# Odd mixer of a hybrid encoder: the forget gate moved into the score matmul, softmax read from PSUM, PSUM banks divided anew

## The chip, the cores and the metric

One core of a Trainium2 chip runs the whole inference step as one program. The metric is the device time of the program in microseconds; a smaller number is better. All times below are for one core, and there is no traffic with other cores.

## The reference, cut to what matters

The model is a two-layer encoder step for a prompt of 512 tokens and a sample of 32 tokens (544 columns side by side), width 1024, everything in float32. Layer 0 has a convolution and state-space mixer, layer 1 (the odd layer) has forgetting attention and a chunk gating unit, and both layers end in a convolutional FFN. The change is in the attention of layer 1: 8 heads of 64 features, in which a cumulated log forget value F is added to the scores.

```python
def fox_block(q, k, v, fq, fk, qpos, kpos):
    s = jnp.einsum('bqhd,bkhd->bhqk', q, k).astype(jnp.float32) * (C_HEAD_DIM ** -0.5)
    s = s + (jnp.transpose(fq, (0, 2, 1))[:, :, :, None] - jnp.transpose(fk, (0, 2, 1))[:, :, None, :])
    s = jnp.where((kpos[None, :] <= qpos[:, None])[None, None], s, MASK_VALUE)
    p = jax.nn.softmax(s, axis=-1)
    return jnp.einsum('bhqk,bkhd->bqhd', p.astype(v.dtype), v)

F = jnp.cumsum(logf.astype(jnp.float32), axis=1)      # logf = log_sigmoid(fl + b_forget)
```

So a score is q.k/8 + F[query] - F[key], masked to keys no later than the query. The prompt is done in blocks of 128 queries, the 32 sample queries see 256 cached keys and their own 32.

## The kernel before, in words

**Products.** Activations lie as (features on partitions, tokens on columns). Every projection goes through `phase` (L163) in jobs: one job is one block of 128 output features on one half of the tokens (256 or 288 columns), 24 matmuls at L128 to L130, because weights and activations are split into a high and a low part (float32r) and three of the four products are formed. A job writes one PSUM bank. Its result is taken out ("drained") by the phase's `consume` function, here `c_in` (L1026), one job later (lag 1). Weights come in blocks of 512 KB: `prefetch` (L91) issues the load on SP's queue (L101, `raw`, two buffers), ScalarE makes the high part `wh` (L104) and VectorE the low part `wl` (L105), four buffers each.

**PSUM.** There are eight banks. The pool `mm` holds four for jobs throughout. In the odd mixer the other four are `sc` with two (scores and other small products), `pp` with one (transposed weights) and `av` with one (weighted values). In the tail (FFN and embedding) `ps_tile` (L110) takes turns between `mm` and three more banks, and one bank serves the norms. In the even mixer the other four go to the state-space scan.

**The odd mixer** (`mixer_odd`, L992) runs 21 weight blocks: the forget logits first, then k, q, v for each of four pairs of heads, then the gating unit's inputs. Beside the jobs run the steps of the attention: `each` (L1332) advances the generator `pipe` (L1182) at a fixed rate per job. There are 16 blocks of the prompt (four pairs, each with four blocks of 128 queries, both heads together) and one block for the sample. At one turn of `pipe` PE gets the weighted values of block t-2, the scores of block t (both heads) and the transposes of the softmax of block t-1.

- `forget` (L1109) makes the log forget values of all heads on 8 partitions and scans them (L1121, L1123) to `F` and `Fs`, the negated sums of prompt and sample. `forget_cols` (L1126) turns them into columns `fq` with small matmuls (L1130, L1134).
- `row` (L1169) copies one head's row of `F` to all 128 partitions, as a DMA on SP's queue from one partition (L1173, tile `Gb`, four buffers, 256 KB each, eight in all); the sample's two `Gb` come by eight smaller ones (L1177). `pipe` issues a row one block before its first use.
- `split_heads` (L1151) splits q or k of a pair into high and low parts (L1159 on ScalarE, L1160 on VectorE) and copies one part to the other 64 partitions with two DMAs issued on POOL (L1163).
- `Head.products` (L1213) forms a head's scores in two passes: 128 rows (q high, q low on k high, k high; L1216), then 64 rows (q high on k low; L1217).
- `Head.softmax` (L1220): VectorE adds `Gb` and the column of `fq` on the way out of PSUM (L1223), adds the mask (L1225), takes the maximum (L1142) and negates it (L1143); ScalarE does the exponential (L1144) and the scaling (L1146), VectorE the reciprocal (L1145).
- `turn` (L1228) transposes the weights (L1231) and ScalarE copies them out (L1233, `pT`, three buffers); `values` (L1235) forms the weighted sum (L1242).
- Around these: `kT` and `vT` go out as results (`out_o_k` at L1047, `out_o_v` at L1052). The gating input `VD` takes the place of `kT` (one buffer), so its first drain (L1043) waits until `out_o_k` has read `kT`. `values_t` (L1069) transposes v through `sc`; ScalarE copies it (L1075).

**Order.** Each engine and each queue works through its instructions in one fixed order. That order is written when the kernel is built, by a scheduler that follows the order of the program and its own estimate of durations, so neighbours on an engine can come from different functions. A wait at the head of an engine or queue holds all that stands behind it.

Of the kernel before, what the change touches and what calls it, by code (L numbers as in the profile page):

```python
# [31 lines left out]
# columns of the packed per-feature parameters  # L32
# [15 lines left out]
# columns of the shape-only constants  # L48
# [3 lines left out]
def units():  # L52
    """Weight blocks in the order of their use: (array, index, K tiles)."""
# [17 lines left out]
def trunk_kernel(ctx: ExitStack, tc: tile.TileContext, A: dict):  # L71
# [36 lines left out]
    psc = {"extra": None, "st": None, "n": 0}  # L108
# [13 lines left out]
    def mm_job(ps, u, ks, xh, xl, c0, n, k0=0):  # L122
        """ps[:, :n] = W.T @ x for one block: W = hi + lo, x = hi + lo."""
# [8 lines left out]
    # ------------------------------------------- work beside the products, in steps  # L132
# [30 lines left out]
    def phase(n, K, src, consume, delta=4, after=(None, None), each=None, rate=2, lag=1):  # L163
        """n weight blocks on both halves of the tokens, the first half ahead by delta."""
# [36 lines left out]
    # -------------------------------------------------------------- constants  # L201
# [15 lines left out]
    act.activation(mhalf, zero[:, 0:4], AF.Gelu_apprx_tanh)      # its table also holds the other functions  # L217
# [6 lines left out]
    # history of the FFN's convolution: [prompt's last two of the first half, cache]  # L224
# [28 lines left out]
    def history(U, half, prev, cache):  # L253
        """The columns before the first token of each block."""
# [56 lines left out]
    def split_x(k, c0, n, src, g=None):  # L311
        """X[k] = src * g in two parts."""
# [7 lines left out]
    def residual(half, h, y, st, gpost, gnext, rB=None):  # L320
        """h += y * g * r; then X of the next projection and, for rB, the norm of h."""
# [37 lines left out]
    def tail(layer, h, next_g):  # L359
        """Output projection of the mixer, FFN and per-layer embedding.  # L360

        X holds the mixer's output. Returns h and rB of the next layer's norm."""
# [3 lines left out]
        psc["extra"] = fs.enter_context(tc.tile_pool(name="fp%d" % layer, bufs=3, space=PSUM))  # L366
# [15 lines left out]
        # the sample's part of the per-layer input  # L382
# [3 lines left out]
        # FFN  # L386
# [57 lines left out]
        # per-layer embedding: half of p @ w_ple  # L444
# [62 lines left out]
    # ------------------------------------------------------- layer 0: the mixer  # L507
    def mixer_even(h):
        ms = ExitStack()
        s5 = ms.enter_context(tc.tile_pool(name="s5", bufs=1))  # L510
        aux = ms.enter_context(tc.tile_pool(name="s5p", bufs=1, space=PSUM))

# [5 lines left out]
        # until their places are filled: bb in the last quarter of Bm, raw in the one before, ct in Tm  # L518
# [11 lines left out]
        # X = h * g, the statistics of h  # L530
# [52 lines left out]
        # ---- discretization, on (2 groups x 64 states, 16 pairs of groups)  # L583
# [29 lines left out]
        def horner(r, cs):  # L613
            """r * (cs[0] + r * (cs[1] + ...))"""
# [16 lines left out]
        pw = s5.tile([128, 5, 2, 16], F32, tag="pw", name="pw")   # powers 1..4 of A  # L631
        pg = s5.tile([128, 2, 16, 3], F32, tag="pg", name="pg")   # powers 3..1, by pair of groups
# [8 lines left out]
        def cmul(o, a, b):  # L641
            """o = a * b, complex"""
# [10 lines left out]
        def discretize():  # L653
# [40 lines left out]
            # f = (A - 1) / a  # L694
# [23 lines left out]
        def rotations():  # L718
            """Powers of the unit rotation per chunk: of column m to m - 63, of the start column and the
            sample's chunks after it to 0, 1, ..."""  # L720
            et = ya.rearrange("p f t -> p (f t)")[:, 0:1024].rearrange("p (a q m) -> p a q m", a=2, q=16)
            for b in range(6):
# [3 lines left out]
                if b in (2, 4, 5):  # L726
                    # back to the unit circle: E *= (3 - |E|^2) / 2
# [22 lines left out]
        # ---- stationary matrices  # L750
# [3 lines left out]
        def prep_b(fr, fi):  # L754
            # bb = ((re, im), (-im, re)) of f * b
# [12 lines left out]
            # raw = ((c_re, -c_im), (-c_im, -c_re))  # L768
# [73 lines left out]
        # ---- chunk scan of two pairs of groups  # L842
# [68 lines left out]
        def shuffle(back_, fs):  # L911
            """Between (channels, time in chunk) and (time in chunk, 2 groups x 16 channels)."""
# [13 lines left out]
        # ---- gated convolution  # L926
# [40 lines left out]
        # ---- gate of the S5 output  # L967
# [7 lines left out]
        for jh in range(2):  # L975
            for o in range(4):
# [7 lines left out]
                for a, b, m0, m1 in ((0, SEQ, 0, 128), (S0, T, SS0, M)):  # L984
# [3 lines left out]
                    vec.scalar_tensor_tensor(xl_, tv[:, :, m0:m1], 0.5, xh_, op0=OP.mult, op1=OP.subtract)  # L988
        ms.close()

    # ------------------------------------------------------- layer 1: the mixer
    def mixer_odd(rB):  # L992
        """Attention and spatial gating."""
# [5 lines left out]
        def sc():  # L999
            return aux.tile([128, 512], F32, tag="sc", name="sc", bufs=2)  # L1000
# [11 lines left out]
        F = at.tile([8, SEQ], F32, tag="F", name="F")               # cumulated log forget, negated  # L1012
        Fs = at.tile([8, 288], F32, tag="Fs", name="Fs")
        fq = at.tile([128, 5, 8], F32, tag="fq", name="fq")
        nid = at.tile([8, 8], F32, tag="nid", name="nid")
        lfs, lf, fa, fb = [uT[0:8, j] for j in range(4)]             # until u is there
# [44 lines left out]
        def spatial():  # L1061
            """The spatial weights (rows s, columns t), of them only s <= t."""
# [6 lines left out]
        def values_t(i):  # L1069
            """v of a pair of heads: (features, tokens) -> (tokens, features)"""  # L1070
# [27 lines left out]
        def to_tokens(src, dst, dst_s, blocks):  # L1098
            """(features, tokens) -> (tokens, features), by blocks of tokens"""
# [405 lines left out]
```

## Time and profile before

| what | value |
|---|---|
| three timed runs | 1452.87, 1453.6, 1455.97 us, median 1453.6 |
| profiled execution, span from first to last instruction | 1451.2 us |
| its own time beside the span | not listed apart; the median of the runs is 2.4 us above the span |
| PE (TensorE matmul) busy | 1384.4 us, 95% |
| VectorE, ScalarE, POOL busy | 960.2, 641.3, 228.8 us |
| odd mixer, first to last job | about 697 to 940 us |

The profile is of one execution. "PE busy" counts matmuls whose ends are modelled; "granted clock" is TensorE's clock as a share of 2.4 GHz, so 0.50 is 1.2 GHz. A wait "A <- B" says that engine A stood idle until B had ended. The chain of waits is the chain of work that ended last, followed back from the end.

### The profile page before, as it was taken

What the parts mean: (1) busy time and instruction counts of PE and PEld (TensorE: products, weight loads), DVE (VectorE), ACT (ScalarE), POOL (GpSimd) and SP (SyncE); (2) the same over time, 40 slices, a digit from 0 to 9 for tenths busy, and PEclk for the clock granted to TensorE, in tenths of its full rate; (3) what the DMA queues carried; (4) which work ended last, traced back from release to release, by engine and by line L of the source; (5) the groups of instructions that cost most, each with busy time, mean ns of one, the idle gap of its engine ahead of it and who ended that gap; (6) DMA issues with size and microseconds to landing.
All of it is one profiled execution on the core that took longest, in us unless ns stands there. A gap on an engine that the chain in (4) does not pass through costs nothing.

```text
span 1451.2 us, 27530 instructions
## 1 busy us (share of the span) xinstructions
PE 1384.4 (95%) x10863; PEld 1352.1 (93%) x10863; DVE 960.2 (66%) x2051; ACT 641.3 (44%) x1268; POOL 228.8 (16%) x658
## 2 busy tenths in 40 slices
PE   8699999999999999999939979999999999999998
PEld 7698999999999999999937868999999999999998
DVE  8998748982578357678506546649881578368683
ACT  6344546552344134465405545556542344134451
POOL 2622000430023002100000000001340024003000
PEclk9899999999999999999968989999999999999999
DMA  5222352231223122241385751231231223122221
GB/s 191 76 65 69 110 184 74 81 110 64 97 83 111 64 94 70 86 139 59 79 60 57 92 146 53 91 118 58 88 131 60 73 88 131 60 73 85 95 83 52
DMA packets 50081, 130.60 MB, mean 90 GB/s; under 512 B 8080, under 2 KB 19736, under 8 KB 49696
## 3 DMA queue, kind: packets, MB, share of 16 engines
q1 hardware_dynamic: 48672, 126.74, 31.0%
q0 software_dynamic: 1280, 2.10, 0.7%
q8 instruction: 85, 1.39, 0.4%
q14 instruction: 44, 0.36, 0.1%
HBM read 116.93 MB, written 4.76 MB: 84 GB/s over the span
## 4 chain that ended last, share of the span: by engine, by line
PE 84%; DVE 8%; DMA 4%; ACT 2%; SPq 2%; issue 1%; POOL 0%; ACTq 0%; DVEq 0%; POOLq 0%
PE ps L128 26%; PE ps L130 26%; PE ps L129 26%; DMA raw<-in_w_odd_in 2%; DMA out_o_k<-kT 1%; DVE wl L105 1%; SPq L1173 1%; PE av L1242 1%; PE sc L1217 1%; PE pp L1231 1%; PE sc L1216 1%; PE rp L298 1%; DVE rg L870 1%; ACT wh L104 0%; DVE y L329 0%
## 5 line engine op out<-in xcount | busy, mean ns | idle before, releaser
L128 PE MATMUL ps<-Xh,wh 128*128 128x256 f32 (+1 forms) x2512 | 730.0, 291 | 6.2 <-DVE UUh L579 5.4
L129 PE MATMUL ps<-Xl,wh 128*128 128x256 f32 (+1 forms) x2512 | 727.6, 290 | 2.6 <-DVE Xl L318 2.4
L130 PE MATMUL ps<-Xh,wl 128*128 128x256 f32 (+1 forms) x2512 | 727.9, 290 | 2.2 <-DVE wl L105 2.2
L128 PEld LDWEIGHTS ps<-Xh,wh 128*128 128x128 f32 x2512 | 476.0, 190 | 9.5 <-issue 3.6
L129 PEld LDWEIGHTS ps<-Xl,wh 128*128 128x128 f32 x2512 | 476.4, 190 | 4.0 <-DVE Xl L318 3.0
L130 PEld LDWEIGHTS ps<-Xh,wl 128*128 128x128 f32 x2512 | 474.9, 189 | 3.3 <-DVE wl L105 2.6
L105 DVE TENSOR_TENSOR wl<-raw,wh 128x1024 fp32r<-128x1024 f32 (+1 forms) x213 | 257.3, 1209 | 183.4 <-ACT wh L104 181.7
L104 ACT ACTIVATE wh<-raw 128x1024 fp32r<-128x1024 f32 (+1 forms) x213 | 221.8, 1042 | 279.8 <-PE ps L129 227.5
L128 PE MATMUL ps<-gh,wh 128*128 128x288 f32 (+1 forms) x704 | 203.5, 289 | 0.0
L130 PE MATMUL ps<-gh,wl 128*128 128x288 f32 (+1 forms) x704 | 203.4, 289 | 0.0
L129 PE MATMUL ps<-gl,wh 128*128 128x288 f32 (+1 forms) x704 | 202.5, 288 | 0.0
L129 PEld LDWEIGHTS ps<-gl,wh 128*128 128x128 f32 x704 | 133.5, 190 | 0.0
L128 PEld LDWEIGHTS ps<-gh,wh 128*128 128x128 f32 x704 | 133.0, 189 | 0.0
L130 PEld LDWEIGHTS ps<-gh,wl 128*128 128x128 f32 x704 | 132.9, 189 | 0.0
L269 ACT ACTIVATE t<-U,prm 128x256 f32<-128x256 f32 (+1 forms) x176 | 90.1, 516 | 71.0 <-DVE U L403 67.5
L270 DVE SCALAR_TENSOR_TENSOR t<-U,prm,t 128x256 f32<-128x256 f32 (+1 forms) x176 | 87.0, 498 | 34.8 <-ACT t L269 34.5
L403 DVE TENSOR_TENSOR U<-ps,rB 128x256 f32<-128x256 f32 (+1 forms) x176 | 76.5, 436 | 24.1 <-PE ps L130 20.3
L271 DVE SCALAR_TENSOR_TENSOR t<-U,prm,t 128x256 f32<-128x256 f32 (+1 forms) x176 | 87.5, 500 | 4.6
L406 POOL COPY hca<-U 128x2 f32<-128x2 f32 x88 | 24.2, 277 | 365.3 <-DVE U L403 365.1
L413 ACT ACTIVATE t<-t 128x288 f32<-128x288 f32 (+1 forms) x88 | 37.6, 428 | 81.6 <-DVE t L271 81.5
L429 DVE TENSOR_TENSOR y<-y,ps 128x256 f32<-128x256 f32 (+1 forms) x64 | 27.9, 437 | 62.1 <-PE ps L130 62.1
L419 ACT ACTIVATE gh<-t 128x288 fp32r<-128x288 f32 (+1 forms) x88 | 37.3, 424 | 67.5 <-DVE t L417 67.5
(276 smaller groups left out, 1427.3 us busy)
## 6 DMA issues: line engine op xcount, KB each, us to landing
raw<-in_w_up SPq DMA_DIRECT2D x88, 512.0 KB, 3.5
raw<-in_w_down SPq DMA_DIRECT2D x32, 512.0 KB, 3.5
raw<-in_w_odd_in SPq DMA_DIRECT2D x21, 512.0 KB, 4.0
raw<-in_w_even_in SPq DMA_DIRECT2D x16, 512.0 KB, 3.6
raw<-in_w_gate SPq DMA_DIRECT2D x16, 512.0 KB, 4.3
raw<-in_w_down SPq DMA_DIRECT2D x16, 384.0 KB, 2.9
raw<-in_w_even_out SPq DMA_DIRECT2D x8, 512.0 KB, 3.9
raw<-in_w_odd_out SPq DMA_DIRECT2D x8, 512.0 KB, 3.5
```

The source lines that it names most:

```text
L104: act.activation(wh[:, :K], raw[:, :K], AF.Copy)
L105: vec.tensor_tensor(wl[:, :K], raw[:, :K], wh[:, :K], op=OP.subtract)
L128: pe.matmul(ps[:, :n], wh[:, k0 + k, :], h_, start=(i == 0), stop=False)
L129: pe.matmul(ps[:, :n], wh[:, k0 + k, :], l_, start=False, stop=False)
L130: pe.matmul(ps[:, :n], wl[:, k0 + k, :], h_, start=False, stop=(i == last))
L269: act.activation(t, v[2], AF.Copy, scale=w(2))
L270: vec.scalar_tensor_tensor(t, v[1], w(1), t, op0=OP.mult, op1=OP.add)
L271: vec.scalar_tensor_tensor(t, v[0], w(0), t, op0=OP.mult, op1=OP.add)
L403: vec.tensor_tensor(block_view(U, half)[2], like(ps, half), like(rB[half], half), op=OP.mult)
L413: act.activation(t, t, AF.Gelu_apprx_tanh)
L419: act.activation(gh[:, f - f0], g, AF.Copy)
L429: vec.tensor_tensor(yk, yk, ps, op=OP.add)
```

## The change

The forget values are no longer copied to all partitions. Per head, 64 partitions of a q tile and of a k tile are free in the first pass; the change puts four useful rows there: q has (F high, F low) against ones in k, and ones against (F high, F low) in k, the rest is zero. So the first pass (q high on k high, plus the gate rows) already holds F[query] - F[key], and the second pass takes both cross terms (q high on k low, q low on k high). The scores are complete in PSUM; mask, maximum and exponential read them there.

- Gone: all 16 row DMAs on SP (L1173, L1177), the addition L1223, the negation L1143 (now in the maximum), the `fq` columns of the prompt, tiles `Gb`, `kl`.
- New: four fixed tiles `QA`, `KA` (two pairs in turn) with 16 memsets on POOL at the mixer's start; `forget` also splits F in two parts twice (`FK`, `FQ`: two ScalarE and two VectorE operations on 8 partitions, written where `lf` lay, which `out_o_logf` reads); per `split_heads` two more small DMAs on POOL (one partition to two, 4 KB; 16 in all); for q two more ScalarE copies of 64x512; `forget_cols` copies the sample's rows by matmul (`Gs`).
- PSUM: `mm` three banks instead of four everywhere; `sc` three instead of two; the tail's second pool four instead of three, with the turns of `ps_tile` turned round so that seven banks still rotate; the even mixer gets one extra bank that takes each fourth job.
- `pT` two buffers instead of three; `F`, `Fs` and a selection matrix use buffers of the pool `S`.

```diff
-    mm = ctx.enter_context(tc.tile_pool(name="mm", bufs=4, space=PSUM))
+    mm = ctx.enter_context(tc.tile_pool(name="mm", bufs=3, space=PSUM))
-        p_ = psc["extra"] if psc["extra"] is not None and psc["n"] % 7 % 2 else mm
+        p_ = psc["extra"] if psc["extra"] is not None and psc["n"] % psc["of"][0] % psc["of"][1] == 0 else mm
-        psc["extra"] = fs.enter_context(tc.tile_pool(name="fp%d" % layer, bufs=3, space=PSUM))
+        psc["extra"] = fs.enter_context(tc.tile_pool(name="fp%d" % layer, bufs=4, space=PSUM))
+        psc["of"] = (7, 2)
...
+        psc["extra"] = ms.enter_context(tc.tile_pool(name="s5m", bufs=1, space=PSUM))
+        psc["of"] = (4, 4)
...
-            return aux.tile([128, 512], F32, tag="sc", name="sc", bufs=2)
+            return aux.tile([128, 512], F32, tag="sc", name="sc", bufs=3)
...
+        FQ, FK = [uT[0:8, j:j + 2, 0:SEQ].bitcast(F32R) for j in (0, 2)]
+        QA, KA = [[at.tile([128, 2, SEQ], F32R, tag="%s%d" % (n, p), name=n) for p in range(2)] for n in ("QA", "KA")]
+        for p in range(2):
+            for hh in range(2):
+                o = gate_rows(hh)
+                pool_e.memset(QA[p][o:o + 32, hh].bitcast(F32), 0.0)
+                pool_e.memset(KA[p][o:o + 32, hh].bitcast(F32), 1.0)
+                pool_e.memset(QA[p][o + 32:o + 64, hh].bitcast(F32), 1.0)
+                pool_e.memset(KA[p][o + 32:o + 64, hh].bitcast(F32), 0.0)
...
-            vec.tensor_tensor_scan(F, one.to_broadcast([8, SEQ]), x[:, 0:SEQ], 0.0, op0=OP.mult, op1=OP.subtract)
+            vec.tensor_tensor_scan(F[0:8], one.to_broadcast([8, SEQ]), x[:, 0:SEQ], 0.0, op0=OP.mult, op1=OP.subtract)
+            act.activation(FK[:, 0], F[0:8], AF.Copy)
+            vec.tensor_tensor(FK[:, 1], F[0:8], FK[:, 0], op=OP.subtract)
...
+            act.activation(FQ[:, 0], F[0:8], AF.Copy, scale=-1.0)
+            vec.tensor_tensor(FQ[:, 1], FK[:, 0], F[0:8], op=OP.subtract)
...
+            for g in range(2):
+                ps = sc()
+                pe.matmul(ps[:, 0:288], pick[:, 128 * g:128 * g + 128], Fs, start=True, stop=True)
...
+            vec.tensor_reduce(mx[:, 1:2], src[:, :n], axis=mybir.AxisListType.X, op=OP.max, negate=True)
+            act.activation(S[:, :n], src[:, :n], AF.Exp, bias=mx[:, 1:2], accum_out=mx[:, 2:3])
...
             for hh in range(2):
-                s, o = slice(hh * 64, hh * 64 + 64), slice(64 - hh * 64, 128 - hh * 64)
-                nc.gpsimd.dma_start(hi[o, hh], lo[s] if isq else hi[s, hh])
...
+                nc.gpsimd.dma_start(B[o:o + 64, hh], lo[s] if isq else A[s, hh])
+                h_ = 2 * i + hh
+                o2 = o if isq else o + 32
+                nc.gpsimd.dma_start(A[o2:o2 + 2, hh], (FQ if isq else FK)[h_:h_ + 1])
...
-        def row(key):
...
-                pe.matmul(ps[:, :n], Q2[i][:, self.hh, b * 128:n], K2[i][:, self.hh, 0:n], start=True, stop=False)
-                pe.matmul(ps[:, :n], Q2[i][s, self.hh, b * 128:n], KL[i][s, 0:n], start=False, stop=True)
+                pe.matmul(ps[:, :n], QA[i % 2][:, hh, b * 128:n], KA[i % 2][:, hh, 0:n], start=True, stop=False)
+                pe.matmul(ps[:, :n], QB[i][:, hh, b * 128:n], KB[i][:, hh, 0:n], start=False, stop=True)
...
-                vec.scalar_tensor_tensor(S[:, :n], Gb[h_][:, :n], fq[:, b, h_:h_ + 1], ps[:, :n],
-                                         op0=OP.add, op1=OP.add)
-                vec.tensor_tensor(S[:, b * 128:n], S[:, b * 128:n], mask_p, op=OP.add)
-                normalize(S, n)
+                vec.tensor_tensor(ps[:, b * 128:n], ps[:, b * 128:n], mask_p, op=OP.add)
+                normalize(S, n, ps)
```

## Rows read from the trace of the kernel before

**Rows 1.** The page's first lines: span, busy time of each engine

```profile
span 1451.2 us, 27530 instructions
...
PE 1384.4 (95%) x10863; PEld 1352.1 (93%) x10863; DVE 960.2 (66%) x2051; ACT 641.3 (44%) x1268; POOL 228.8 (16%) x658
```

**Rows 2.** Waits by engine and line, 700 to 900 us: total, times, longest

```profile
ACT wh L104 <- DMA raw<-in_w_odd_in: 32.6, 2, 32.4
...
PE sc L1216 <- ACT VT L1075: 26.2, 1, 26.2
...
DVE VD L1043 <- DMA out_o_k<-kT: 12.7, 1, 12.7
...
PE pp L1231 <- ACT pT L1233: 11.5, 1, 11.5
```

**Rows 3.** Chain that ended last, 690 to 930 us: start, length, what

```profile
726.37 9.96 SPq L1173
736.44 24.27 DMA raw<-in_w_odd_in
...
763.70 0.48 PE sc L1216
...
821.47 20.92 DMA out_o_k<-kT
...
845.01 0.47 PE pp L1231
```

**Rows 4.** What the DMA engines moved, 715 to 765 us in 40 slices

```profile
GB/s 29 341 170 134 29 26 28 26 26 26 26 33 26 26 26 28 28 26 62 129 61 41 30 29 31 29 28 43 26 28 26 28 26 26 280 243 252 82 2 267
```

**Rows 5.** Stretches: length, busy by engine (PE first), granted clock, DMA share, GB/s

```profile
770.00:771.00 1.00, 1.00 (x8) 1.00 (x8) 0.00 (x0) 0.00 (x0) 0.00 (x0) 0.73 0.00 0
...
849.00:850.00 1.00, 1.00 (x10) 0.87 (x11) 0.18 (x1) 0.00 (x0) 1.00 (x2) 0.97 0.85 283
...
864.00:866.00 2.00, 2.00 (x18) 2.00 (x18) 0.62 (x2) 1.77 (x4) 0.67 (x1) 1.00 0.78 31
```

**Rows 6.** In order of time: VectorE's first drain of VD; SP's issue of out_o_v

```profile
842.49 0.42 DVE L1043 SCALAR_TENSOR_TENSOR VD<-ps,rB 128x256 f32<-128x256 f32 x1 [12.66 <-DMA out_o_k<-kT]
...
856.28 0.34 SPq L1052 DMA_DIRECT2D out_o_v<-vT  x1
```

**Rows 7.** Groups of instructions by shape, 690 to 900 us: busy, mean ns

```profile
L1223 DVE SCALAR_TENSOR_TENSOR S<-Gb,fq,sc 128x512 f32<-128x512 f32 x8 | 5.9, 746 | 2.5 <-PE sc L1217 1.4 <-PE pp L1231 1.1
...
L1159 ACT ACTIVATE hi<-qT 64x512 fp32r<-64x512 f32 x8 | 5.0, 623 | 0.1
...
L1216 PE MATMUL sc<-hi 128*128 128x512 f32 x8 | 4.0, 498 | 0.0
L1217 PE MATMUL sc<-lo,hi 64*128 64x512 f32 x8 | 4.0, 498 | 0.0
```

**Rows 8.** PE in order of time: forget columns; scores at a pair's start

```profile
718.39 1.05 PE L1130 MATMUL sc<-nid,F 8*128 8x8 f32 x8 [0.76 <-DVE F L1121]
720.51 0.30 PE L1134 MATMUL sc<-nid,Fs 8*32 8x1 f32 x16
...
825.09 0.33 PE L1216 MATMUL sc<-hi 128*128 128x128 f32 x1
...
827.44 0.38 PE L1217 MATMUL sc<-lo,hi 64*128 64x256 f32 x1
```

**Rows 9.** POOL: the longest memset's group, then two rows in order of time

```profile
L525 POOL MEMSET Cm<- 128x5120 f32 x1 | 4.4, 4365 | 0.0
...
703.60 0.85 POOL L302 TENSOR_TENSOR rc<-mc,mhalf 128x3 f32<-128x3 f32 x1 [18.20 <-DVE mc L300]
...
725.23 0.51 POOL L1163 DMA_DIRECT2D hi<-lo  x1 [0.21 <-issue]
```

**Rows 10.** Issue to landing: the copies of L1163, then the rows of L1173

```profile
DMA to landing us min/median/max: 2.2/3.3/23.7
...
DMA to landing us min/median/max: 11.8/15.8/34.1
```

More of the change, by code (lines that the diff above doesn't have):

```diff
@@ L988, in mixer_even @@
                     vec.scalar_tensor_tensor(xl_, tv[:, :, m0:m1], 0.5, xh_, op0=OP.mult, op1=OP.subtract)
+        psc["extra"] = None
         ms.close()
@@ L1011, in mixer_odd, with gate_rows @@
         bs = at.tile([128, 4, 128], F32, tag="bs", name="bs")
-        F = at.tile([8, SEQ], F32, tag="F", name="F")
-        Fs = at.tile([8, 288], F32, tag="Fs", name="Fs")
-        fq = at.tile([128, 5, 8], F32, tag="fq", name="fq")
+        F, Fs = buf("F"), buf("Fs")[0:8, 0:288]
+        Gs = []
         nid = at.tile([8, 8], F32, tag="nid", name="nid")
+        FQ, FK = [uT[0:8, j:j + 2, 0:SEQ].bitcast(F32R) for j in (0, 2)]
+        QA, KA = [[at.tile([128, 2, SEQ], F32R, tag="%s%d" % (n, p), name=n) for p in range(2)] for n in ("QA", "KA")]
+        def gate_rows(hh):
+            return 64 - hh * 64
+        for p in range(2):
[5 more added lines that the diff above has]
+                pool_e.memset(KA[p][o + 32:o + 64, hh].bitcast(F32), 0.0)
         lfs, lf, fa, fb = [uT[0:8, j] for j in range(4)]
@@ L1124, in forget @@
                                    op0=OP.mult, op1=OP.subtract)
+            act.activation(FQ[:, 0], F[0:8], AF.Copy, scale=-1.0)
+            vec.tensor_tensor(FQ[:, 1], FK[:, 0], F[0:8], op=OP.subtract)
         def forget_cols():
             yield True
-            ps = sc()
-            for b in range(4):
-                pe.matmul(ps[:, b * 8:b * 8 + 8], F[:, b * 128:b * 128 + 128], nid,
-                          start=True, stop=True)
-            for h_ in range(8):
-                g, r = divmod(h_, 4)
-                pe.matmul(ps[32 * r:32 * r + 32, 32 + g:33 + g], Fs[:, 256:288], nid[:, h_:h_ + 1],
-                          start=True, stop=True, tile_position=(0, 32 * r))
@@ L1136, in forget_cols @@
-            act.activation(fq[:, 0:4].rearrange("p b h -> p (b h)"), ps[:, 0:32], AF.Copy)
-            act.activation(fq[:, 4, 0:2], ps[:, 32:34], AF.Copy)
+            pick = buf("pick")[0:8, 0:256]
+            act.activation(pick.rearrange("p (h q) -> p h q", q=32),
+                           ident[0:8, 0:8][:, :, None].to_broadcast([8, 8, 32]), AF.Copy)
+            for g in range(2):
+                ps = sc()
+                pe.matmul(ps[:, 0:288], pick[:, 128 * g:128 * g + 128], Fs, start=True, stop=True)
+                for r in range(4):
+                    h_ = 4 * g + r
+                    pe.matmul(ps[32 * r:32 * r + 32, 288:289], Fs[:, 256:288], nid[:, h_:h_ + 1],
+                              start=True, stop=True, tile_position=(0, 32 * r))
+                Gs.append(at.tile([128, 289], F32, tag="Gs%d" % g, name="Gs"))
+                act.activation(Gs[g], ps[:, 0:289], AF.Copy)
@@ L1145, in normalize @@
             vec.reciprocal(mx[:, 3:4], mx[:, 2:3])
             act.activation(S[:, :n], S[:, :n], AF.Copy, scale=mx[:, 3:4])
-        Gb, av = {}, {}
-        Q2, K2, KL = {}, {}, {}
+        av = {}
+        QB, KB = {}, {}
         def split_heads(i, isq):
-            hi = at.tile([128, 2, SEQ], F32R, tag="q2" if isq else "k2", name="hi", bufs=2)
-            lo = at.tile([128, SEQ], F32R, tag="S" if isq else "kl", name="lo", bufs=4 if isq else 2)
+            A, B = (QA if isq else KA)[i % 2], at.tile([128, 2, SEQ], F32R, tag="q2" if isq else "k2", name="B", bufs=2)
@@ L1156, in split_heads @@
             src = (qT if isq else kT)[:, i, 0:SEQ]
+            lo = at.tile([128, SEQ], F32R, tag="S", name="lo", bufs=4) if isq else None
             for hh in range(2):
                 s = slice(hh * 64, hh * 64 + 64)
-                act.activation(hi[s, hh], src[s], AF.Copy)
-                vec.tensor_tensor(lo[s], src[s], hi[s, hh], op=OP.subtract)
+                act.activation(A[s, hh], src[s], AF.Copy)
+                vec.tensor_tensor(lo[s] if isq else B[s, hh], src[s], A[s, hh], op=OP.subtract)
+                if isq:
+                    act.activation(B[s, hh], src[s], AF.Copy)
@@ L1161, in split_heads @@
             for hh in range(2):
-                s, o = slice(hh * 64, hh * 64 + 64), slice(64 - hh * 64, 128 - hh * 64)
-                nc.gpsimd.dma_start(hi[o, hh], lo[s] if isq else hi[s, hh])
-            if isq:
-                Q2[i] = hi
-            else:
-                K2[i], KL[i] = hi, lo
-        def row(key):
-            g = Gb[key] = at.tile([128, SEQ], F32, tag="Gb", name="Gb", bufs=4)
-            if key < 8:
-                nc.sync.dma_start(g, F[key:key + 1][:, None].to_broadcast([1, 128, SEQ]))
-            else:
-                for r in range(4):
-                    h_ = 4 * (key - 8) + r
-                    nc.sync.dma_start(g[32 * r:32 * r + 32, 0:288], Fs[h_:h_ + 1][:, None].to_broadcast([1, 32, 288]))
+                s, o = slice(hh * 64, hh * 64 + 64), gate_rows(hh)
@@ L1187, in pipe @@
                 if t < NB:
-                    for x in blocks[t]:
-                        if x.h not in Gb:
-                            row(x.h)
                     ps = [x.products() for x in blocks[t]]
@@ L1193, in pipe @@
                         x.softmax(p_)
-                    if t + 1 < len(blocks):
-                        for x in blocks[t + 1]:
-                            if x.h not in Gb:
-                                row(x.h)
                 if 1 <= t < NB + 1:
@@ L1231, in turn @@
                     pe.transpose(pp[:, k * 128:k * 128 + 128], self.S[:, k * 128:k * 128 + 128], ident)
-                self.pT = at.tile([128, SEQ], F32, tag="pT", name="pT", bufs=3)
+                self.pT = at.tile([128, SEQ], F32, tag="pT", name="pT", bufs=2)
                 act.activation(self.pT[:, :self.n], pp[:, :self.n], AF.Copy)
@@ L1266, in softmax @@
                 S = self.S = buf("S")
[L1267 removed]
+                vec.scalar_tensor_tensor(S[:, 0:288], Gs[g][:, 0:288], Gs[g][:, 288:289], ps[:, 0:288],
                                          op0=OP.add, op1=OP.add)
@@ L1275, in turn @@
                     pe.transpose(pp[:n, k * 128:k * 128 + 128], self.S[:, k * 128:k * 128 + n], ident)
-                self.pT = at.tile([128, SEQ], F32, tag="pT", name="pT", bufs=3)
+                self.pT = at.tile([128, SEQ], F32, tag="pT", name="pT", bufs=2)
                 act.activation(self.pT[:, 0:256], pp[:, 0:256], AF.Copy)
```

14 lines of the change are left out of this document (6 added, 8 removed).

## The prediction

> **What bounds the kernel now.** I read the page first. PE is busy 1384.4 of 1451.2 us [rows 1], so TensorE sets the pace, and a change to the attention's other engines can only pay where PE stands still. The next view is therefore the waits of the odd mixer. Two waits of PE stand out there [rows 2]: 26.2 us in front of the first scores (L1216) and 11.5 us in front of transposes (L1231). The line named as releaser, a ScalarE copy, is only the last link. The same view shows what held ScalarE and VectorE: ScalarE's weight split L104 waited 32.4 us for a weight load, and VectorE's first drain of `VD` waited 12.7 us for the output copy `out_o_k`.
>
> The chain of waits says why these two transfers were late [rows 3]. Before the weight load stands SP itself, held by the issue of the broadcast rows L1173 (the last of the first four took 9.96 us to issue), so the load went out only at 736.44, and then it took 24.27 us to land. What filled the DMA engines is seen in the rates [rows 4]: for most of 40 us they moved 26 to 29 GB/s, though the weight loads before and after show 243 to 341. A row copy reads one partition and lands after 11.8 to 34.1 us [rows 10]. The second case has the same pattern: two rows were issued just before `out_o_k`, which needed 20.92 us [rows 3]. So both stalls come from the broadcasts of F, through SP's queue and through the DMA engines.
>
> **The change, part by part.**
>
> *Broadcasts gone.* The four first rows no longer stand between two weight loads on SP, and nothing slow lies in front of the load. The first idle ends at 763.70 [rows 3]; it began 26.2 us earlier, at 737.5, and I take all of it as gained. The second, 11.5 us, likewise. What is late next? For the weights: PE's next job with that block cannot start before the scores that PE waited for, and an unhindered load lands in a few us, so nothing. For `out_o_k`: VectorE came to the drain at 842.49 - 12.66 = 829.83 [rows 6], that is 8.4 us after the issue at 821.47. `out_o_v`, the same size, was issued at 856.28 [rows 6] with two 512 KB loads beside it, and by 864 the rate had fallen to 31 GB/s [rows 5]; that is under 8 us. So the wait is 0 to 2 us on VectorE, and PE had other work until 833.5: nothing.
>
> *Clock.* After each idle stretch PE worked at 1.2 GHz for a while. In the slice from 770 to 771 the mean granted clock was 0.73, so full speed came at about 770.54; in that from 849 to 850 it was 0.97, so at 849.06 [rows 5]. PE ran at half clock from 763.70 to 770.54 (6.84 us) and from 845.01 [rows 3] to 849.06 (4.05 us). At full clock that work takes half: 3.4 and 2.0 us gained.
>
> *PE's own work.* The second pass contracts 128 rows instead of 64; both passes took 498 ns for 512 columns [rows 7], so nothing. `forget_cols` now needs the second scan for all its matmuls. Before, PE waited 0.76 us for the first scan, at 718.39, and came to the group that needs the second at 720.51 [rows 8]. The added wait is at most 2.1 us and at least nothing; I take 1.5, near the top, because two operations for the split of F now lie between the scans.
>
> *Softmax from PSUM.* VectorE loses L1223 (746 ns at 512 columns [rows 7]) and a one-column operation; the maximum and the mask read PSUM now, and even if each cost as much as L1223 did, no more would come back than left. ScalarE gets eight more copies at 623 ns for q [rows 7], 5.0 us in all. Over the span VectorE is busy 66% and ScalarE 44% [rows 1], so this lies beside PE's work: nothing. A bank with scores is now held until the exponential has read it, not until the first VectorE operation. The place to look is a pair's start, where four score tiles follow each other from 825.09 to 827.8 [rows 8]. The third bank takes one; the fourth tile needs the bank of the first, about 2 us after that was filled, and mask, maximum and exponential take about that. Between 0 and 1 us for each of four pairs: I take 0.5, so 2 us.
>
> For this the Trainium skill (PSUM — Partial Sum Buffer, Summary: rules for kernel authors) says to empty PSUM promptly because it is small, which speaks against reading a softmax from it. By that rule every block would wait, as in the second rival below; by the rows only pair starts do.
>
> *Banks of the jobs.* Three instead of four in the odd mixer. With lag 1 a job needs the bank of the job three before; nearly all drains start as their job ends, apart from the two stalls, and a late one has two whole jobs as cover. In tail and even mixer seven and four banks rotate as before. Nothing.
>
> *POOL.* 16 memsets of 512 columns at 4365/5120 ns per column [rows 9] are 0.44 us each, 7.0 in all. Behind them stands the norm's power at 703.60, before which POOL idled for 18.2 us [rows 9]; with the mixer's memory free at its first job, near 697, they end near 704, and that power, 0.85 us long, is wanted one job later. Nothing; were the memory free only at 703.6, up to 7.0 us. Two more DMA issues of 0.51 us [rows 9] per split put the last one for pair 0 at 725.74 + 1.0 = 726.8, still 10.7 us ahead of the scores at 737.5. VectorE's `FQ` overwrites what `out_o_logf` reads and waits for it; behind it stand drains of two jobs, covered by the third bank. Nothing.
>
> *Sum.* -26.2 - 11.5 - 3.4 - 2.0 + 1.5 + 2 = -39.6 us. The profiled span of 1451.2 becomes 1411.6; the median of the runs is 2.4 us above the span, so I forecast 1414.0 us.
>
> **Rivals.**
>
> 1. *The second stall stays*: `out_o_k` still lands late, because loads go out beside it. For: a 1 MB output and loads share the engines. Against: `out_o_v` under the same load. It keeps 11.5 + 2.0 us: 1427.5.
> 2. *Scores wait for banks at every block*: the exponential stands behind other ScalarE work, and PE waits 1 us for each of 17 blocks instead of 2 us in all. For: the longer hold. Against: after a pair's start at least a job's products lie between two blocks. It costs 15 us: 1429.
> 3. *Slower: the gate rows arrive late.* They too are read from one partition, and go through POOL's queue. If such a row landed like a broadcast, after 34.1 us [rows 10], each pair's first scores would wait, taken at pair 0's margin, 34.1 - 10.7 = 23.4 us, four times: 1414.0 + 94 = 1508. It decides from a landing of about 20.6 us on (39.6/4 = 9.9 beyond the margin). For: even a copy of L1163 once took 23.7 us. Against: that was under the broadcasts; the least is 2.2 us for 128 KB [rows 10], and a gate row has 4 KB.
> 4. *The broadcasts are not what held the transfers*, so both stalls stay: 1453.6 + 3.5 = 1457 at most, or the same as now. Against: the rates [rows 4].
>
> **How the numbers follow.** The forecast has 0.75, rival 1 0.10, rival 2 0.09, rival 3 0.03, rival 4 0.03. Low end: no added waits (-3.5), and PE's small wait of 0.76 us [rows 8] and the bubbles between a 128-row and a 64-row pass go too (some 4 us by an estimate of 0.1 us for each of 32 tiles): 1406. High end: rivals 1 and 2, 1430. About 0.1 is left out above and below. A measurement of this kernel tells 0.2%, 2.9 us, from no change. Faster by more than that: forecast, rivals 1 and 2, 0.94. Within it: 0.02. Slower: 0.04.
>
> **What would show it.** Right: no stretch of half clock between 700 and 930 us, the weight load landing in under 6 us, no wait of VectorE for `out_o_k` over 2 us, odd mixer some 40 us shorter, tails unchanged. PE's waits before the scores would be under 1 us each, and at pair starts only. Wrong: a new wait of PE for score banks or for gate rows at each pair, a wait of the job's matmuls for a bank, or tails that take longer under the new turns of the banks.

## The result, and the profile after

The changed kernel takes **1403.99 us**, median of four runs (1403.22 to 1404.62), against 1453.23 us before (four runs, 1452.81 to 1455.97): a ratio of 0.9657, with a 95% interval of 0.9643 to 0.967. Its profiled execution took 1403.22 us around a span of 1401.5 us, 49.7 us less than the span of [rows 1]. The forecast was 1414.0 with a range from 1406 to 1430: the direction and the cause of the two stalls were right, the gain was about 10 us larger than forecast, and the result lies just below the low end.

The page's first lines of the changed kernel, to be read against [rows 1]:

```profile
span 1401.5 us, 27494 instructions
...
PE 1369.6 (98%) x10859; PEld 1346.7 (96%) x10859; DVE 945.0 (67%) x1987; ACT 645.6 (46%) x1279; POOL 244.2 (17%) x690
```

TensorE is now busy for 98% of the span. But its busy time also fell, by 14.8 us, although it contracts more rows than before. Halved half-clock work explains 3.4 + 2.0 us of that by the prediction's own terms; the rest was the first sign that a term was missing.

The waits of PE from 690 to 940 us in the changed kernel (engine, line, releaser: us in total, times, longest), to be read against [rows 2]:

```profile
PE sc L1226 <- ACT S L1168: 1.6, 4, 1.2
PE sc L1155 <- ACT pick L1151: 1.3, 1, 1.3
```

The waits of 26.2 and 11.5 us are gone. What is left is one wait at the mixer's start (L1155, `forget_cols`), and four waits of scores (L1226) for a bank, one at each pair's start: 1.2 us at the first, 0.15 to 0.16 us at the others.

The row of the first wait names ScalarE's `pick`, a selection matrix, but by its times that had ended at 719.42. VectorE's second scan ended at 720.02, just before PE went on at 720.12, so it was the scan that PE waited for, as the prediction had it:

```profile
719.27 0.75 DVE L1143 TENSOR_TENSOR_SCAN Fs<-ones,uT 8x288 f32<-8x288 f32 x1
```

What the DMA engines of the changed kernel moved from 715 to 765 us, in 40 slices, and the weight loads of that stretch (times issued, KB, median us to landing), to be read against [rows 4]:

```profile
GB/s 16 252 248 139 0 5 8 3 52 334 218 35 0 0 92 341 0 0 11 231 349 38 0 0 0 0 0 92 321 125 51 66 2 0 0 85 315 20 0 0
...
raw<-in_w_odd_in SPq DMA_DIRECT2D x7, 512.0 KB, 4.3
```

The plateau at 26 to 29 GB/s is gone. The engines now work in short bursts of up to 349 GB/s and then stand idle, and weights land in 4.3 us.

Where the time went can be laid out along the mixer, since each job's products are drained by VectorE in both kernels. The table gives the start of the same drain in both traces (line L1043 before, L1061 after):

| drain (tile, columns, which) | before, us | after, us | gained so far |
|---|---|---|---|
| kT, 288, first | 712.96 | 713.07 | -0.1 |
| kT, 288, second | 733.51 | 735.86 | -2.4 |
| vT, 256, third | 787.17 | 759.02 | 28.2 |
| kT, 288, fourth | 820.99 | 790.12 | 30.9 |
| VD, 256, fourth | 867.80 | 821.09 | 46.7 |
| uT, 288, fifth | 926.64 | 877.32 | 49.3 |

All of the gain lies inside the odd mixer. Its start loses 2.4 us; the two stretches with the former stalls give 30.5 and 15.8 us; and two stretches that never had a stall (787 to 821, and 868 to 927 by the clock of before) still give 2.7 and 2.6 us. These last are what the sum did not have. Each of the four stretches holds 16 of the 64 score passes of the prompt, so of the 30.5 and 15.8 us some 2.6 us each may belong to them too.

### The profile page after: what moved, and what is told of

The parts are those of the page before. It is cut to its first block, busy times and chain, and to the rows that moved or that the text cites. A ratio compares the mean times of both kernels' runs of the same rounds, so it can differ in the third digit from the quotient of the medians.

```text
span 1401.5 us, 27494 instructions
## 1 busy us (share of the span) xinstructions
PE 1369.6 (98%) x10859; PEld 1346.7 (96%) x10859; DVE 945.0 (67%) x1987; ACT 645.6 (46%) x1279; POOL 244.2 (17%) x690
## 3 DMA queue, kind: packets, MB, share of 16 engines
q1 hardware_dynamic: 47136, 124.35, 27.9%
## 4 chain that ended last, share of the span: by engine, by line
PE 88%; DVE 8%; ACT 2%; issue 1%; DMA 1%; POOL 0%; SPq 0%; ACTq 0%; DVEq 0%; POOLq 0%
PE ps L128 27%; PE ps L129 27%; PE ps L130 27%; DVE wl L105 1%; PE av L1250 1%; PE rp L298 1%; PE pp L1239 1%; DVE Xl L318 1%; PE sc L1226 1%; DVE rg L873 0%; PE yp L890 0%; PE tp L836 0%; DVE y L329 0%; ACT wh L104 0%; PE tb L822 0%
## 5 line engine op out<-in xcount | busy, mean ns | idle before, releaser
L430 DVE TENSOR_TENSOR y<-y,ps 128x256 f32<-128x256 f32 (+1 forms) x64 | 27.9, 436 | 62.1 <-PE ps L130 62.1
L302 POOL TENSOR_TENSOR rc<-mc,mhalf 128x2 f32<-128x2 f32 (+1 forms) x18 | 15.1, 838 | 306.8 <-DVE mc L300 298.5
```

The source lines that it names most:

```text
L430: vec.tensor_tensor(yk, yk, ps, op=OP.add)
```

## A first look at the gap: matmuls by their starts

The row of a matmul has a modelled end, so its length says little. The time from one start to the next says more. PE in order of time, scores of two heads over 384 columns, first before the change (start us, us, engine, line, out<-in, weight tile, columns):

```profile
803.25 0.44 PE L1216 MATMUL sc<-hi 128*128 128x384 f32 x1
803.63 0.44 PE L1217 MATMUL sc<-lo,hi 64*128 64x384 f32 x1
804.00 0.43 PE L1242 MATMUL av<-pT,VT 128*64 128x128 f32 x2
804.36 0.44 PE L1216 MATMUL sc<-hi 128*128 128x384 f32 x1
804.73 0.44 PE L1217 MATMUL sc<-lo,hi 64*128 64x384 f32 x1
805.10 0.44 PE L1231 MATMUL pp<-cst,S 128*128 128x128 f32 x2
```

and in the changed kernel:

```profile
774.22 0.44 PE L1226 MATMUL sc<-KA,QA 128*128 128x384 f32 x1
774.50 0.34 PE L1227 MATMUL sc<-B 128*128 128x384 f32 x1
774.67 0.34 PE L1226 MATMUL sc<-KA,QA 128*128 128x384 f32 x1
774.85 0.34 PE L1227 MATMUL sc<-B 128*128 128x384 f32 x1
775.02 0.38 PE L1239 MATMUL pp<-cst,S 128*128 128x128 f32 x2
...
775.60 0.28 PE L128 MATMUL ps<-Xh,wh 128*128 128x256 f32 x1
775.72 0.28 PE L129 MATMUL ps<-Xl,wh 128*128 128x256 f32 x1
```

The last two rows are the yardstick: 256 columns in 0.12 us. By it 384 columns take 0.18 us. After the change three of the four passes are followed 0.17 to 0.18 us after their start, and the first one after 0.28. Before, each of the four was followed only after 0.37 to 0.38 us, some 0.2 us more than its columns at each edge where the weight tile goes from 128 rows to 64 or back. The rows differ less in length (0.44 us against 0.34 to 0.44), and [rows 7] gave the two passes of before the same 498 ns, because both carried the same extra.

## The experiments

The theory after this look: the two stalls come from the broadcasts of F, and the extra gain comes from TensorE no longer changing between 128-row and 64-row contractions. The rival for the extra gain: softmax out of PSUM, the gate rows or the banks.

**Before, with 128 rows in the second pass.**

```
-pe.matmul(ps[:, :n], Q2[i][s, self.hh, b * 128:n], KL[i][s, 0:n], start=False, stop=True)
+pe.matmul(ps[:, :n], Q2[i][:, self.hh, b * 128:n], KL[i][:, 0:n], start=False, stop=True)
```

> The kernel before with one edit: the second score pass contracts all 128 rows (q hi on k lo, and q lo on the other head's k lo, a product of two remainders) instead of the 64 rows of its head. Instructions, columns, transfers and both stalls stay. Theory A (TensorE loses time at each change between a 128-row and a 64-row contraction; in the trace of before the next start came some 0.2 us after the columns of either pass were through, in the changed kernel some 0.08 us): 32 blocks x 2 changes x 0.13 to 0.19 us = 8 to 12 us less, 1441 to 1445 us. Rival B (the score passes cost by their columns alone, and the gain beyond the two stalls comes from the softmax out of PSUM or the PSUM banks): within 0.2% of before, 1450 to 1456.

Measured: 1444.39 us against 1453.23, ratio 0.9942 (0.993 to 0.9955), so 8.8 us less with both stalls in place. Its PE waits, 690 to 940 us:

```profile
PE sc L1216 <- ACT VT L1075: 24.6, 1, 24.6
PE pp L1231 <- ACT pT L1233: 11.8, 1, 11.8
```

Its passes, now of one shape, over 512 columns:

```profile
807.75 0.50 PE L1216 MATMUL sc<-hi 128*128 128x512 f32 x1
808.08 0.39 PE L1217 MATMUL sc<-lo,hi 128*128 128x512 f32 x1
808.31 0.39 PE L1216 MATMUL sc<-hi 128*128 128x512 f32 x1
808.54 0.39 PE L1217 MATMUL sc<-lo,hi 128*128 128x512 f32 x1
```

The last three start 0.23 us apart, as their columns ask; the first pass of the step is followed after 0.33 us here too. Added up over all 64 score passes of the prompt, at that pace for the columns and at full clock, the time from each start to the next holds some 12 us beyond the columns in the kernel before, and some 3.6 us here (estimates from the two traces, with idle waits left out). So a pass of 128 rows between others of 128 rows costs less than one of 64. Rival B is out.

**After, with 64 rows in the second pass.**

```
-pe.matmul(ps[:, :n], QB[i][:, hh, b * 128:n], KB[i][:, hh, 0:n], start=False, stop=True)
+pe.matmul(ps[:, :n], QB[i][self.s, hh, b * 128:n], KB[i][self.s, hh, 0:n], start=False, stop=True)
```

> The changed kernel with one edit: the second score pass contracts the 64 rows of its head alone, as before the change; it leaves out q lo on k hi, so the scores are coarser. Softmax out of PSUM, banks, gate rows and transfers stay as changed. Theory A (changes between 128-row and 64-row contractions): 8 to 12 us more than the changed kernel, 1412 to 1416 us. Rival B: as the changed kernel, 1402 to 1406.

Measured: 1412.69 us, ratio to before 0.9721 (0.9708 to 0.9735): 8.7 us more than the changed kernel. The term is the same from either side.

**The same, with the passes in another order.** Is a 64-row pass slow, or the change to it?

```
 ps = [x.products() for x in blocks[t]]
+if t < 16:
+    for x, p_ in zip(blocks[t], ps):
+        x.second(p_)
...
-pe.matmul(ps[:, :n], QB[i][:, hh, b * 128:n], KB[i][:, hh, 0:n], start=False, stop=True)
...
+    pe.matmul(ps[:, :n], QB[i][s, hh, b * 128:n], KB[i][s, hh, 0:n], start=False, stop=True)
```

> The changed kernel with the 64-row second pass of e4_after_64rows (q lo on k hi left out), and besides the order of the four passes of a pair of heads changed: both 128-row passes first, then both 64-row passes, so two changes of contraction per pair of heads and not four, with the same instructions. Theory A (each change costs): about half of the 8.7 us that the 64 rows cost comes back, 1407 to 1410 us; if the change from rows 0-63 to rows 64-127 costs as much as one from 128 to 64, three changes, 1410 to 1411. Rival C (a 64-row pass is slow by itself, not the change): no difference to e4_after_64rows, 1412 to 1414.

Measured: 1408.11 us, ratio 0.9679 (0.9666 to 0.9692): of the 8.7 us, 4.6 came back from the order alone (by the ratios, as the kernel before was measured anew beside this run, 6.1 of 9.3 us). PE in order of time, four passes of 128 columns, first in the kernel with alternating shapes:

```profile
769.69 0.33 PE L1226 MATMUL sc<-KA,QA 128*128 128x128 f32 x1
769.95 0.33 PE L1227 MATMUL sc<-B 64*128 64x128 f32 x1
770.20 0.33 PE L1226 MATMUL sc<-KA,QA 128*128 128x128 f32 x1
770.46 0.32 PE L1227 MATMUL sc<-B 64*128 64x128 f32 x1
770.71 0.66 PE L1239 MATMUL pp<-cst,S 128*128 128x128 f32 x4
```

then in the regrouped one (x2: two passes in one row):

```profile
768.16 0.44 PE L1229 MATMUL sc<-KA,QA 128*128 128x128 f32 x2
768.53 0.33 PE L1234 MATMUL sc<-B 64*128 64x128 f32 x2
768.78 0.66 PE L1245 MATMUL pp<-cst,S 128*128 128x128 f32 x4
```

The four take 1.02 us alternating and 0.62 us grouped. Two things go into this. There are fewer changes, and the two 64-row passes, one on rows 0-63 and the other on rows 64-127, run side by side: both are through in 0.25 us (768.53 to 768.78), the time that one alone takes in the kernel with alternating shapes (769.95 to 770.20).

In the trace this happens in 11 of the 16 steps. In the others the scheduler put other products between, so 42 changes of row count are left, not 32. The overlap is worth some 1.8 us, an estimate from the columns of one pass in each of the 11 steps, at the pace of the yardstick. With it one change comes to (1408.11 - 1403.99 + 1.8) / 42 = 0.14 us; the alternating kernel gives 8.7 / 64 = 0.14 us (by the ratios 0.12 and 0.15). This is the net of what goes away: an edge shows some 0.2 us, but the first pass of a step is late in one shape too, for a reason that no run here looks for.

The order alone does not put rival C out, since the overlap would also hide a pass that is slow by itself. The starts speak against it: a 128-row pass of 384 columns was followed by a 64-row one after 0.37 to 0.38 us, and in the changed kernel by a 128-row one after 0.18 to 0.28 us, so a part of the extra stands ahead of the 64-row pass. The Trainium skill says the same (TensorEngine Tiling (Array Packing), Key Properties): to change the tiling mode, and not merely the tile, drains TensorE. The trace agrees, with some 0.2 us at an edge.

**Before, without the broadcasts.**

```
+        G0 = at.tile([128, SEQ], F32, tag="Gb", name="G0", bufs=4)
+        pool_e.memset(G0, 0.0)
...
-            g = Gb[key] = at.tile([128, SEQ], F32, tag="Gb", name="Gb", bufs=4)
...
+            Gb[key] = G0
```

> The kernel before without the ten broadcasts of F: all heads and the sample add one tile of zeros in their place, so the scores lack -F of the key; every DVE, ACT and PE instruction of the softmax stays. Theory A (the broadcasts alone cause both idle stretches, as the prediction had it): both go, 29.6 + 13.5 us by the prediction's terms with their half clock, 1409 to 1413 us; the rest of the changed kernel's gain stays away. Rival (what holds the transfers is the weights and outputs themselves): 1445 or more.

Measured: 1411.02 us, ratio 0.9708 (0.9693 to 0.9723), 42.2 us less. The prediction's terms for the two stalls with their half clock, 26.2 + 11.5 + 3.4 + 2.0 = 43.1 us, hold, and the broadcasts alone are their cause.

**Before, with the rows from DRAM.** What is it about the broadcasts?

```
-nc.sync.dma_start(g, F[key:key + 1][:, None].to_broadcast([1, 128, SEQ]))
+nc.sync.dma_start(g, A["x"][key:key + 1, 0, 0:SEQ].to_broadcast([128, SEQ]))
...
```

> The kernel before with the ten broadcasts read from DRAM (a row of the input x, so the scores get wrong gate values) and no longer from one SBUF partition; count, sizes, destination, queue and order of the transfers stay. Theory A1 (the single source partition is what makes them slow, 26 to 31 GB/s while they ran): the broadcasts land in a few us, both idle stretches go or nearly go, 1409 to 1418 us. Rival A2 (128 or 32 descriptors of 1 to 2 KB to 128 partitions on one queue are slow whatever their source): the idle stretches stay, 1445 to 1455.

Measured: 1410.15 us, ratio 0.9706 (0.9693 to 0.9719). Ten broadcasts of the same size on the same queue (eight rows and the sample's two tiles), and no stall. One thing did not stay as the expectation has it. A row of x need not wait for F, so the first four rows went out from 698.6 us on and not from 718.4, well ahead of the load that was late before; for the first stall this is no clean comparison (the kernel with F by way of DRAM, below, is one). The last two rows still went out just before `out_o_k`, which landed in 4.7 us, and VectorE did not wait for it. Issue to landing of its row copies (us), to be read against [rows 10]:

```profile
DMA to landing us min/median/max: 3.0/5.3/7.0
```

**Before, with copies from 128 partitions.** The source is SBUF again.

```
-nc.sync.dma_start(g, F[key:key + 1][:, None].to_broadcast([1, 128, SEQ]))
+nc.sync.dma_start(g, vC[:, 0])
...
```

> The kernel before with the ten broadcasts turned into copies of a tile of cached values from SBUF, each of the 128 (or 32) destination partitions read from its own source partition; so the scores get wrong gate values. Destination, sizes, queue and order stay; the source is SBUF still, but no longer one partition. Theory S (one source partition read 128 times over is what is slow): the copies land in 3 to 6 us and both idle stretches go, 1409 to 1414 us. Rival (SBUF as a source, beside weights on their way, is slow): landings of 10 us or more and idle stretches left, 1430 or more.

Measured: 1413.11 us, ratio 0.9715 (0.9698 to 0.9732). Its DMA issues, 700 to 900 us (times, KB each, median us to landing):

```profile
Gb<-vC SPq DMA_DIRECT2D x8, 256.0 KB, 2.5
```

2.5 us against 15.8 in [rows 10]. (Here too the first four went out early, from 704.3 us on.) So it is the one source partition, not SBUF as a source, nor the copy to 128 partitions. The Trainium skill has the rate (SBUF — State Buffer, Door 1: The DMA port swizzle): four partitions behind one port gave 27.6 GB/s. The plateau of [rows 4], 26 to 29 GB/s, agrees.

**Before, with the broadcasts on POOL's queue.**

```
-nc.sync.dma_start(g, F[key:key + 1][:, None].to_broadcast([1, 128, SEQ]))
+nc.gpsimd.dma_start(g, F[key:key + 1][:, None].to_broadcast([1, 128, SEQ]))
...
```

> The kernel before with one edit: the ten broadcasts of F, still from the one SBUF partition, are issued on POOL's queue and no longer on SP's, where the weights and outputs are issued. Theory Q (order on the queue: a weight behind a broadcast on the same queue waits for it): both idle stretches go or nearly go, 1409 to 1420 us, unless the halves of the heads that POOL also copies come late. Theory E (the broadcasts fill the DMA engines themselves, whatever queue they come by; in the trace of before 54% of the engines' time from 700 to 900 us went to SP's queue): weights and outputs still land late, 1435 to 1460.

Measured: 1454.39 us, ratio 1.0 (0.999 to 1.001). Nothing is gained. What the DMA engines moved from 715 to 765 us, and two kinds of issues there (median us to landing):

```profile
GB/s 0 229 264 154 61 23 29 26 26 29 23 23 26 33 23 49 33 56 33 62 43 52 36 62 33 59 46 59 36 39 43 36 46 36 123 305 211 89 0 72
...
raw<-in_w_odd_in SPq DMA_DIRECT2D x4, 512.0 KB, 17.8
Gb<-F POOLq DMA_DIRECT2D x4, 256.0 KB, 26.3
```

The weights, with no broadcast on their queue, still take 17.8 us to land in that stretch. The load that PE's scores had to wait for went out at 724.35, 12 us earlier than in [rows 3], and landed at 761.6, no earlier than there (760.7). So the slow copy holds the DMA engines themselves. The prediction had named both SP's queue and the engines; the queue's part is not needed.

**After, with the old PSUM division.**

```
-mm = ctx.enter_context(tc.tile_pool(name="mm", bufs=3, space=PSUM))
+mm = ctx.enter_context(tc.tile_pool(name="mm", bufs=4, space=PSUM))
...
-            return aux.tile([128, 512], F32, tag="sc", name="sc", bufs=3)
+            return aux.tile([128, 512], F32, tag="sc", name="sc", bufs=2)
```

> The changed kernel with the PSUM division of before: four common banks, two for scores, three more for the tails, none more for the even mixer. Softmax straight from PSUM, gate rows and all else as changed. Theory A (two score banks come free before the next pair of heads' blocks need them in nearly every step, since some 8 us of products lie between): the changed kernel's time or up to 3 us more, 1403 to 1407. Rival D (softmax out of PSUM holds two banks too long, the prediction's second rival): a wait of 0.5 us or more at most of the 16 steps and half a clock behind some, 1412 or more.

Measured: 1404.57 us, ratio 0.966 (0.9647 to 0.9673), the changed kernel's time. Its PE waits for a score bank:

```profile
PE sc L1224 <- ACT S L1166: 1.7, 3, 1.3
```

With four banks for the jobs beside them, two score banks do as well as three, and the rival in which every block waits has no support.

**After, with the products on F later.** The wait at L1155 had a second price. Stretches of the changed kernel (length, busy by engine with PE first, granted clock, DMA share, GB/s):

```profile
721.00:722.00 1.00, 1.00 (x12) 0.46 (x11) 0.53 (x1) 0.41 (x1) 0.91 (x2) 0.71 0.01 2
722.00:723.00 1.00, 1.00 (x8) 1.00 (x5) 0.15 (x1) 0.81 (x2) 0.95 (x2) 0.50 0.06 6
723.00:724.00 1.00, 1.00 (x7) 1.00 (x6) 0.61 (x2) 1.00 (x2) 0.54 (x2) 0.50 0.06 8
724.00:725.00 1.00, 1.00 (x7) 1.00 (x7) 1.00 (x2) 0.99 (x3) 0.00 (x0) 0.58 0.03 4
```

After the 1.3 us of idle PE, the clock stands at half of 2.4 GHz from about 721.4 to 724.8. The slices sum to 0.29 + 0.50 + 0.50 + 0.42 = 1.7 us of lost full-clock time. It does not always come to that: behind the 1.2 us in which the first pair's scores waited, up to 742.24, the granted clock is 1.00 from 740 to 748, and in the trace of the kernel with alternating 64-row passes the same wait at L1155 is followed by a clock of 1.00 from 721 to 726. So the products on F go later:

```
+pick = VS[0:8, 1, 0:256]
...
 if half == 1:
     forget()
-    task(forget_cols())
 return
+if i == 2 and half == 1:
+    task(forget_cols())
...
+act.activation(VS[0:8, 1, 256:257], ones[0:8, 0:1], AF.Exp)
```

> The changed kernel with the gate matrix for the sample (pick) made at the start of the mixer in a place that is free there, the ten products on F moved two feature blocks later, behind the second query block, and one Exp on ACT behind them that brings its table in before the first softmax. Nothing is left out. Theory A (the start of the mixer costs 1.3 us of idle PE before the products on F and about 1 to 1.6 us of half clock behind it): both go, 2 to 4 us less than the changed kernel, 1400 to 1402. Rival (the idle time is taken over by the next wait): 1403 to 1405.

Measured: **1400.19 us**, ratio to before 0.9628 (0.9615 to 0.9641), 3.8 us less than the changed kernel. The run moves three things at once and does not tell them apart. The rows above give 1.3 + 1.7 us of it, and PE's waits for score banks are 0.6 us shorter (1.0 against 1.6). The same stretch shows full clock, for example:

```profile
722.00:723.00 1.00, 1.00 (x10) 1.00 (x9) 1.00 (x2) 0.89 (x2) 0.95 (x2) 1.00 0.06 8
723.00:724.00 1.00, 1.00 (x10) 1.00 (x9) 0.86 (x3) 0.99 (x3) 0.00 (x0) 1.00 0.06 8
```

**Before, with 128 rows and F by way of DRAM.** Do the two causes make up the whole?

```
...
+nc.gpsimd.dma_start(Fd[:, 0:SEQ], F)
+nc.gpsimd.dma_start(Fd[:, SEQ:SEQ + 288], Fs)
...
-nc.sync.dma_start(g, F[key:key + 1][:, None].to_broadcast([1, 128, SEQ]))
+nc.sync.dma_start(g, Fd[key:key + 1, 0:SEQ].to_broadcast([128, SEQ]))
...
-pe.matmul(ps[:, :n], Q2[i][s, self.hh, b * 128:n], KL[i][s, 0:n], start=False, stop=True)
+pe.matmul(ps[:, :n], Q2[i][:, self.hh, b * 128:n], KL[i][:, 0:n], start=False, stop=True)
```

> The kernel before with two edits: the 128-row second pass of e1_before_128rows, and F and Fs written once to a scratch in DRAM, from which the ten broadcasts read the true values. Softmax by DVE out of PSUM into SBUF, column of F, banks stay as before; nothing is left out. Theory A (the two causes are all of the gain and add up: -8.8 and -43.1 us): 1400 to 1403 us, so that softmax straight from PSUM, the gate rows and the banks of the change bring nothing of their own. Rival (they bring part of the changed kernel's time): above 1405.

Measured: 1401.74 us, ratio 0.9639 (0.9625 to 0.9653). Two small edits of the old kernel reach the changed kernel's time; the intervals of the two overlap, so which is faster is not told apart. Its rows wait for F, as before, and the first four go out from 720.99 us on, among the weight loads. Neither stall is there, so this kernel gives the clean comparison for the first one. The rows' issues, 700 to 900 us:

```profile
Gb<-Fd SPq DMA_DIRECT2D x8, 256.0 KB, 3.8
```

**The same, with the products on F later.**

> The kernel of e8_before_128rows_F_in_dram with the products on F moved two feature blocks later and one Exp behind the scans, as in e7_after_gate_columns_later. Nothing is left out. By the same step of the sum as there: the 0.8 us of idle PE before the products on F go, and what half clock stood behind them: 1 to 2 us less than e8's 1401.7, 1399.5 to 1401. If softmax straight from PSUM and the gate rows bring anything of their own, e7_after_gate_columns_later (1400.2) stays below it; if not, the two are within 1 us of each other.

The edit is the last one of the changed kernel's variant, put into this one. Measured: 1400.03 us, ratio 0.9628 (0.9614 to 0.9642), equal to that variant's 0.9628. Softmax straight from PSUM, the gate rows and the new banks bring nothing of their own that these runs can tell; each interval is some 2 us wide to either side.

## Why the prediction was wrong by 10 us

*Broadcasts gone, and the clock: right.* Forecast 29.6 us for the first stall with its half clock, the table shows 30.5; for the second 13.5, the table shows 15.8. Without some 2.6 us of each for its score passes, 27.9 and 13.2 us are left for the stalls (estimates). The kernel without broadcasts, otherwise that of before, gives 42.2 against 43.1. `out_o_k` no longer holds VectorE, as argued.

*PE's own work: the step that failed.* It said "both passes took 498 ns for 512 columns [rows 7], so nothing". The two equal lengths were taken for equal cost, but a matmul's row has a modelled end, and the 0.2 us between the end of one pass's columns and the start of the next lay inside both. Measured: 8.8 us less from this part alone in the kernel of before, 8.7 us more when it is undone in the changed one. The prediction priced "the bubbles between a 128-row and a 64-row pass" only for its low end, at 0.1 us for each of 32 tiles together with a small wait, and no row stands behind the 0.1; there are two changes for each tile, at 0.14 us: 9 us. With this term the sum is 1414.0 - 8.8 = 1405.2, within 1.2 us of the result.

*The wait of `forget_cols`: too small.* Forecast +1.5 us; the table has 2.4. The wait itself was in bounds (1.3 us, 0.6 more than before). What the step left out is the half clock behind it, 1.7 us in this execution.

*Score banks: the sum about right, its parts not.* Forecast 0.5 us at each of four pair starts; measured 1.2 us at the first and 0.15 to 0.16 us at the three others, 1.6 us in all. That the sums are close is luck. For the rule that PSUM should be emptied promptly (the Trainium skill, PSUM — Partial Sum Buffer, Summary: rules for kernel authors), from which the second rival came, no run here shows a cost beyond such waits: with two banks and a softmax that reads them the time is the same.

*What it said would show it.* Weights land in 4.3 us (under 6), both waits are gone, and the gain comes from the odd mixer alone. "No stretch of half clock between 700 and 930" did not hold, at 721 to 725, nor did "under 1 us each" for the waits before the scores, with 1.2 us at the first pair.

None of the four rivals came about. The gate rows, which also leave one partition, are small (4 KB against 256 KB) and landed in 1.6 to 1.8 us at the median, from 715 to 765 us.

## What to carry to other kernels

Read matmul cost from start to start, against a row whose cost is plain, and look for gaps where the weight tile's row count changes: fill up a short contraction with harmless rows, or group passes of one shape. A row that is to reach all partitions should not be read 128 times from one SBUF partition. A trip through DRAM was three to four times faster here, and a product that brings the row in needs no copy to 128 partitions; another queue did not help, since the slow copy holds the engines. A small wait of TensorE costs its own length and can cost a stretch of half clock behind it, so work that nobody needs yet belongs later.

## What was not expected of the hardware

- More rows made the product faster: 128 rows instead of 64 saved 8.8 us, 0.14 us net for each change of shape that went away.
- Two 64-row passes on different halves of the rows ran side by side: both were through in the 0.25 us that one takes alone.
- A broadcast from one partition slows transfers of other queues too: issued on POOL's queue it cost as much time (1454.39 us against 1454.56 in the same comparison), with weights on SP's queue landing after 17.8 us at the median.
- A broadcast read from DRAM took 3.8 to 5.3 us at the median, a quarter to a third of the 15.8 us from one SBUF partition.
